# Attention scores of 128 queries computed as two halves of 64 queries by 192 keys

## The chip, the core and the metric

The kernel runs on one core of a Trainium2 chip. A core has a tensor engine (PE in the profile; its weight loads are listed apart as PEld), a vector engine (DVE), a scalar engine (ACT), GpSimd (POOL) and a sync engine (SP) that issues most transfers; 16 DMA engines move the data. The metric is device time in microseconds (us) of the one core, the median of several executions, and lower is better.

## The reference

One inference step of a small decoder: a pooling layer, then an attention layer, over a prompt of 1024 tokens and 8 single decode tokens, all in fp32 with a model width of 2048. The part that matters here is the attention of the prompt. There are 32 query heads of 64 dimensions over 4 key/value heads, and the window is 128: in blocks of 128 queries, each query sees keys of its own block up to itself and keys of the block before that are less than 128 back.

```python
def attn_core(q, k, v, q_pos, k_pos, sinks):
    s = jnp.einsum('...qkgd,...skd->...kgqs', q, k).astype(jnp.float32) * (HEAD_DIM ** -0.5)
    qp = q_pos[..., :, None]
    kp = k_pos[..., None, :]
    mask = (kp <= qp) & (qp - kp < WINDOW) & (kp >= 0)
    s = jnp.where(mask[..., None, None, :, :], s, NEG)
    sink = sinks.astype(jnp.float32).reshape(N_KV_HEADS, GROUP)[:, :, None, None]
    m = jnp.maximum(jnp.max(s, axis=-1, keepdims=True), sink)
    p = jnp.exp(s - m)
    p = p / (jnp.sum(p, axis=-1, keepdims=True) + jnp.exp(sink - m))
    return jnp.einsum('...kgqs,...skd->...qkgd', p.astype(v.dtype), v)
```

The keys of a block of 128 queries are 256: the 128 of the block before (slots 0 to 127) and its own 128 (slots 128 to 255). Query i of the block may use slot k of the block before only where k > i, and slot k of its own only where k <= i, so exactly 128 of the 256 scores of a query are used.

## The kernel before

The tokens are worked on in two chunks of 512 and 520 (512 prompt tokens and 8 decode tokens). The large projections are matrix products with fp32 operands split into a high and a low part, three products each (lines 654 to 656 of `seven`, a Strassen scheme with seven block products; lines 682 to 684 of `unit`, a plain scheme for two short stages). The phases run in the order of the table `PHASES`: "ai" (input projection of the pooling layer), "ao" (its output), "bi" (key/value, query and gate projections of the attention layer, with the attention itself between them), "bo" (its output), each for chunk 0 and chunk 1. The first half of "bi" for chunk 0 is a plain phase, the rest Strassen.

The order on PE, DVE and ACT is the order of the source: `in_order` chains each instruction of these three engines to the one before it. SP's and POOL's queues are left to the scheduler of the framework. What work of the attention goes where between the projections is written out with counters: `self.at(n, go)` runs `go` n steps of the projection later, `self.product(n, rank, go)` does the same for work on PE, at the end of a step. Each `end()` closes a step.

`attend` handles two heads (one tile of 128 channels, head j in partitions 64j to 64j+63) over the four blocks of a chunk. Its pieces: `score` (line 1755) multiplies queries by keys into the PSUM tile `S`, of 2 by 1024 floats per partition, head j in half j, block b in columns 256b to 256b+255. `select` (line 1772, ACT) copies slots 0 to 127 of each block out of `S`; `largest` (line 1776, DVE) copies the block's own slots over them where the mask `mki` says k <= i, so that 128 scores are left for each query, and takes the maximum; exponentials and division follow (lines 1789 to 1804); `turn` (line 1808, PE) transposes the result back into `S`; `keep` (lines 1817 and 1818) copies it out; `values` (line 1832, PE) multiplies by the values, for head j into partitions 64j to 64j+63, and `gate` (line 1841) multiplies with the gate. There are 16 calls of `attend` per chunk, 32 in all.

`S` is made once, when the "bi" stage of chunk 0 opens (`use_four(False)`); `kv_open` sets up the key and value tiles there. The first other writer of `S` is `v_done` (line 1681), which transposes values into half 0; decode scores use `S` too (line 1926).

The prediction also speaks of line 593 (an ACT operation on the Strassen accumulators that PE waits for), line 1620 (rotary embedding on DVE), lines 490 and 774 (DVE, low parts of weights and activations), line 1966 (values of the decode tokens).

Of the kernel before, what the change touches and what calls it, by code (L numbers as in the profile page):

```python
# [16 lines left out]
P = 128  # L17
# [164 lines left out]
class Kern:  # L182
# [1439 lines left out]
    def kv_open(self, c):  # L1622
        nc = self.nc
        T = CHUNKS[c][1]
        if c == 0:
            self.kv = [self.mem.full() for _ in range(4)]
            A, B, C, Dd = (s.a for s in self.kv)
            self.kT = [A[:, :640], B[:, :640]]
            self.vd = B[:, 640:896]
            self.V = [A[:, 640:896]] + [C[:, b * 256 : (b + 1) * 256] for b in range(4)]  # L1630
            self.Vd = [Dd[:, b * 256 : (b + 1) * 256] for b in range(4)]
            for k in self.kT:
                nc.gpsimd.memset(k[:, 0:P], 0.0)
            nc.gpsimd.memset(self.V[0], 0.0)
            self.rt = self.mem.full()
        else:

            def over():
                for k in self.kT:
                    nc.scalar.copy(k[:, 0:P], k[:, TP : TP + P])  # L1640
                nc.scalar.copy(self.V[0], self.V[NB])

            self.at(6, over)
        self.rtab = self.rt.v(2, TMAX)
        nc.sync.dma_start(self.rtab[:, :, :T], self.io[f"rt{c}"])
# [95 lines left out]
    def attend(self, c, t, at, s1, s2, late=False):  # L1741


        nc = self.nc
# [5 lines left out]
        def score():  # L1750
            s, q, lastq = self.qs.pop((c, t))
            for b in range(NB):
                for j in range(2):
                    r = slice(64 * j, 64 * j + 64)
                    nc.tensor.matmul(  # L1755
                        self.S[:, j, b * 256 : b * 256 + 256], q[r, b * P : (b + 1) * P],
                        self.kT[t // 8][r, b * P : b * P + 256], start=True, stop=True,
                    )
            if lastq:
                s.free()  # L1760

# [76 lines left out]
        def gate():  # L1838
# [13 lines left out]
            if j == 1 or t == 15 or self.sg.get((c, t + 1), (None,))[0] is not z:  # L1852
                z.free()

        self.product(at, 2, score)
        for n, go in enumerate((
            select, largest, lambda: expo(0), lambda: expo(1), total, lambda: norm(0), lambda: norm(1)
# [466 lines left out]
```

## Time and profile before

| | |
|---|---|
| median of 3 runs | 2366.13 us (2365.59 to 2367.04) |
| the profiled execution, its own time | 2367.1 us |
| its span, first to last instruction | 2365.3 us |
| mean granted TensorE clock | 0.997 |
| PE busy | 98% of the span |
| DVE busy | 81% |
| ACT busy | 58% |
| score products, line 1755 | 512 matmul records, 63.9 us busy |

Times in the profile are us from the start of the span unless marked ns. A matmul's record is longer than the time after which the next one can start, since matmuls are pipelined; the pace is therefore read from starts, not from durations. In a row of the timeline, "x16" says that 16 instructions of one line that follow each other are merged: the first number is the start of the first, the second the time to the end of the last. Shapes such as "64\*128 64x256" of a matmul mean: weights of 64 rows (partitions) and 128 columns, moving data of 64 partitions by 256 elements.

### The profile page before, as it was taken

The numbers are of one execution on the slowest core, as the hardware profiler recorded it, in microseconds if no ns is written. First come the engines' busy times: TensorE is split into PE (matmuls) and PEld (weight loads), VectorE is DVE, ScalarE is ACT, GpSimd is POOL, SyncE is SP. The second block draws the span as 40 slices with busy tenths as digits, with TensorE's granted clock in tenths as the row PEclk, the third lists the DMA queues.
The fourth block names the chain that finished last, engine by engine and source line by source line (L and its number), as shares of the span: only waits on it lengthen the run. The fifth ranks groups of instructions, "written<-read, shape, count | busy, mean of one in ns | idle before, by whom it ended". The sixth has DMA issues, their size and how long they took to land. (4 is left out here: it accounts for less than half of the span.)

```text
span 2365.3 us, 46576 instructions
## 1 busy us (share of the span) xinstructions
PE 2325.4 (98%) x18424; PEld 2218.8 (94%) x18424; DVE 1922.8 (81%) x2385; ACT 1364.2 (58%) x2502; POOL 201.8 (9%) x379
## 2 busy tenths in 40 slices
PE   8999999999999999999999999999999999999997
PEld 6899999999999999998778899999999999999997
DVE  8788988776878878868888897887777767888887
ACT  4454446544546547554554666675666678556656
POOL 0111110001000000000111111100000000000000
PEclk9999999999999999999999999999999999999999
DMA  8668789989879889989789776788776768699785
GB/s 292 214 243 303 269 289 340 338 286 321 294 279 363 320 279 326 336 313 330 280 317 332 258 239 216 242 290 269 240 256 220 225 191 296 229 350 362 272 303 194
DMA packets 252060, 669.19 MB, mean 283 GB/s; under 512 B 25760, under 2 KB 106560, under 8 KB 251840
## 3 DMA queue, kind: packets, MB, share of 16 engines
q1 hardware_dynamic: 206368, 501.14, 63.0%
q0 software_dynamic: 45472, 165.07, 18.0%
q8 instruction: 144, 2.36, 0.4%
q14 instruction: 76, 0.62, 0.1%
HBM read 471.01 MB, written 185.59 MB: 278 GB/s over the span
## 5 line engine op out<-in xcount | busy, mean ns | idle before, releaser
L654 PE MATMUL pD<-m,m 128*128 128x260 f32 (+1 forms) x4752 | 1346.1, 283 | 7.9 <-ACT pD L593 5.7
L656 PE MATMUL pD<-m,m 128*128 128x260 f32 (+1 forms) x4752 | 1340.2, 282 | 6.9 <-DVE m L490 6.8
L655 PE MATMUL pD<-m,m 128*128 128x260 f32 (+1 forms) x4752 | 1339.5, 282 | 0.9 <-DVE m L774 0.9
L654 PEld LDWEIGHTS pD<-m,m 128*128 128x128 f32 x4752 | 895.1, 188 | 18.6 <-issue 8.0
L656 PEld LDWEIGHTS pD<-m,m 128*128 128x128 f32 x4752 | 895.7, 188 | 9.2 <-DVE m L490 9.2
L655 PEld LDWEIGHTS pD<-m,m 128*128 128x128 f32 x4752 | 895.5, 188 | 1.6 <-DVE m L774 1.1
L490 DVE TENSOR_TENSOR m<-m,m 128x1024 fp32r<-128x1024 f32 x674 | 814.4, 1220 | 87.2 <-ACT m L475 55.1
L475 ACT CAST m<-m 128x1024 fp32r<-128x1024 f32 x674 | 703.6, 1048 | 266.2 <-DVE m L333 66.6
L682 PE MATMUL pD<-m,m 128*128 128x512 f32 x448 | 179.9, 402 | 8.1 <-ACT m L765 8.1
L683 PE MATMUL pD<-m,m 128*128 128x512 f32 x448 | 177.5, 396 | 0.5 <-DVE m L774 0.5
L684 PE MATMUL pD<-m,m 128*128 128x512 f32 x448 | 177.5, 396 | 0.0
L774 DVE TENSOR_TENSOR m<-m,m 128x1024 fp32r<-128x1024 f32 (+1 forms) x120 | 147.2, 1228 | 7.4 <-ACT m L765 6.0
L765 ACT CAST m<-m 128x1024 fp32r<-128x1024 f32 (+1 forms) x120 | 125.8, 1053 | 15.0 <-PE pD L683 5.2
L615 DVE TENSOR_TENSOR m<-pD,m 128x260 f32<-128x260 f32 (+1 forms) x86 | 36.6, 425 | 107.5 <-ACT pD L614 100.0
L627 ACT COPY m<-pD 128x260 f32<-128x260 f32 (+1 forms) x83 | 31.0, 374 | 153.4 <-PE pD L656 153.4
L682 PEld LDWEIGHTS pD<-m,m 128*128 128x128 f32 x448 | 84.8, 189 | 30.0 <-ACT m L765 8.1
L333 DVE TENSOR_TENSOR m<-m,m 128x1024 f32<-128x1024 f32 x88 | 107.6, 1222 | 5.8 <-DMA m<-in_wia 4.3
L683 PEld LDWEIGHTS pD<-m,m 128*128 128x128 f32 x448 | 84.9, 190 | 19.9 <-DVE m L774 1.0
L684 PEld LDWEIGHTS pD<-m,m 128*128 128x128 f32 x448 | 84.8, 189 | 19.9
L1791 ACT ACTIVATE m<-m,sm 128x128 f32<-128x128 f32 x256 | 99.2, 390 | 0.0
L1084 PE MATMUL pD<-m,m 128*128 128x260 f32 (+1 forms) x528 | 91.5, 323 | 0.0
L1084 PEld LDWEIGHTS pD<-m,m 128*128 128x128 f32 x528 | 79.5, 188 | 8.2
(244 smaller groups left out, 2151.4 us busy)
## 6 DMA issues: line engine op xcount, KB each, us to landing
m<-in_wia SPq DMA_DIRECT2D x124, 512.0 KB
m<-in_wib SPq DMA_DIRECT2D x120, 512.0 KB
swia<-m POOLq DMA_DIRECT2D x64, 512.0 KB, 4.8
m<-swia SPq DMA_DIRECT2D x64, 512.0 KB
m<-swoa SPq DMA_DIRECT2D x64, 512.0 KB
swib<-m POOLq DMA_DIRECT2D x64, 512.0 KB, 5.2
m<-swib SPq DMA_DIRECT2D x64, 512.0 KB
m<-swob SPq DMA_DIRECT2D x56, 512.0 KB
```

Of the source, the lines that this page charges most:

```text
L333: self.nc.vector.tensor_add(s[out].a[:, :1024], s[x].a[:, :1024], s[y].a[:, :1024])
L475: self.nc.scalar.copy(hi.r[:, :1024], self.stream[self.cast].src().a[:, :1024])
L490: self.nc.vector.tensor_sub(lo.r[:, :1024], s.src().a[:, :1024], hi.a[:, :1024])
L654: nc.tensor.matmul(ps[:, :TH], wh[:, s], h, start=new and k == 0, stop=False, skip_group_check=on)
L655: nc.tensor.matmul(ps[:, :TH], wh[:, s], l, start=False, stop=False, skip_group_check=on)
L656: nc.tensor.matmul(ps[:, :TH], wl[:, s], h, start=False, stop=k == 7, skip_group_check=on)
L682: nc.tensor.matmul(ps[:], wh[:, s], h, start=par == 0 and k == 0, stop=False)
L683: nc.tensor.matmul(ps[:], wh[:, s], l, start=False, stop=False)
L684: nc.tensor.matmul(ps[:], wl[:, s], h, start=False, stop=par == 1 and k == 7)
L765: self.nc.scalar.copy(h.r[:, :n], s.a[:, :n])
L774: self.nc.vector.tensor_sub(l.r[:, :n], s.a[:, :n], h.a[:, :n])
L1084: nc.tensor.matmul(ps[:, : cs.stop - cs.start], ws[:, s], d[:, cs], start=f0 and k == 0, stop=l0 and k == 3,)
```

## The change

Each product of 128 queries by 256 keys is replaced by two: queries 0 to 63 by slots 0 to 191, and queries 64 to 127 by slots 64 to 255. Head j lies in partitions 64j to 64j+63 of the operands, half a of the queries in partitions 64a to 64a+63 of the result, so the four combinations of j and a use four different quarters (64 rows by 64 columns) of the PE array. For each block there are four such products where there were two. The scores left out are those of queries 0 to 63 with slots 192 to 255 and of queries 64 to 127 with slots 0 to 63. None of them is used by the mask; the places in `S` keep what was there. `select` still copies slots 0 to 127 of all queries, and `largest` overwrites the old content in slots 0 to 63 of the upper queries. So that nothing unset is read, half 1 of `S` is set to zero once by DVE, 4 steps after the stage opens.

```diff
@@ kv_open, chunk 0 @@
             for k in self.kT:
                 nc.gpsimd.memset(k[:, 0:P], 0.0)
+            self.at(4, lambda: nc.vector.memset(self.S[:, 1, :], 0.0))
             nc.gpsimd.memset(self.V[0], 0.0)
@@ attend, score @@
             for b in range(NB):
                 for j in range(2):
                     r = slice(64 * j, 64 * j + 64)
-                    nc.tensor.matmul(
-                        self.S[:, j, b * 256 : b * 256 + 256], q[r, b * P : (b + 1) * P],
-                        self.kT[t // 8][r, b * P : b * P + 256], start=True, stop=True,
-                    )
+                    for a in range(2):
+                        h, k = 64 * a, b * P + 64 * a
+                        nc.tensor.matmul(
+                            self.S[h : h + 64, j, b * 256 + h : b * 256 + h + 192], q[r, k : k + 64],
+                            self.kT[t // 8][r, k : k + 192], start=True, stop=True,
+                        )
```

## The prediction

> **What bounds the kernel now.** I read the head of the page first, then the busy time of the engines over the attention stage, cut in three, and what PE waited for there.
>
> ```profile
> PE 2325.4 (98%) x18424; PEld 2218.8 (94%) x18424; DVE 1922.8 (81%) x2385; ACT 1364.2 (58%) x2502; POOL 201.8 (9%) x379
> ```
>
> ```profile
> core 0: us, PE busy (x) PEld busy (x) DVE busy (x) ACT busy (x) POOL busy (x), PEclk, DMA share, GB/s
> 1150.00:1345.00 195.00, 193.51 (x1059) 155.61 (x1058) 169.06 (x237) 110.75 (x261) 33.95 (x66) 1.00 0.85 305
> 1345.00:1610.00 265.00, 260.77 (x2335) 251.96 (x2335) 230.38 (x275) 181.97 (x413) 28.24 (x56) 1.00 0.74 251
> 1610.00:2060.00 450.00, 447.08 (x4035) 432.68 (x4034) 330.50 (x428) 303.13 (x704) 24.41 (x39) 1.00 0.72 236
> ```
>
> ```profile
> PE pD L654 <- ACT pD L593: 3.6, 4, 1.2
> PE pS L1755 <- DVE m L1727: 1.5, 1, 1.5
> PE pD L656 <- DVE m L490: 0.9, 2, 0.5
> ```
>
> PE is the bound. Over these 910 us it is idle for 1.49 + 4.23 + 2.92 = 8.6 us; DVE, the next, is busy 87%, 87% and 73% of the three windows, no transfer is among PE's longer waits, and the clock is granted in full. So PE time saved on the scores is device time, except where PE soon waits for another engine anyway. Such places lie in the second window.
>
> **What a burst of scores costs now.** The first rows below give all records of line 1755; the others are rows of the PE timeline: two bursts with what follows them, and, from narrow windows, starts inside the first burst of all.
>
> ```profile
> L1755 PEld LDWEIGHTS pS<-m,m x512: 182/187/187, 1159.1 to 2009.9; 64*128 64x128 f32 x171
> L1755 PE MATMUL pS<-m,m x512: 376/376/481, 1159.1 to 2010.1; 64*128 64x256 f32 x171
> ```
>
> ```profile
> 1159.40 0.59 PE L1755 MATMUL pS<-m,m 64*128 64x256 f32 x3
> 1159.62 0.59 PE L1755 MATMUL pS<-m,m 64*128 64x256 f32 x3
> ...
> 1160.48 0.59 PE L1755 MATMUL pS<-m,m 64*128 64x256 f32 x3
> ...
> 1675.61 1.97 PE L1832 MATMUL pO<-m,m 128*64 128x128 f32 x32
> 1677.50 2.00 PE L1755 MATMUL pS<-m,m 64*128 64x256 f32 x16
> 1679.43 0.39 PE L654 MATMUL pD<-m,m 128*128 128x260 f32 x1
> ```
>
> 512 records over 32 calls are 16 per burst, where the code issues 8 products: an fp32 product is two passes. A burst holds PE from 1677.50 to 1679.43, 1.93 us. A record takes 376 ns; 16 in a row would be 6.0 us. Starts inside the burst come 0.22 us apart (1159.40, 1159.62), five steps taking 1.08 us (1159.40 to 1160.48), so a step is 0.216 us. Eight steps are 1.73 us: two records go in each step, one per head, on the upper and the lower half of the array's rows, and 1.93 - 1.73 = 0.20 us are filling and draining. The value products of line 1832 halve the array the other way (weights of 128 rows by 64 columns): 32 records of 128 moving columns in 1.89 us (1675.61 to 1677.50). In 16 steps of two that is at most 1.89 / 16 = 0.118 us a step, or 0.108 if a step costs half of 0.216 for half the columns; one by one they would need at least 32 times that, some 3.5 us. So two halves of rows do run together, and so do two halves of columns.
>
> **The change, part by part.**
>
> *The scores.* Per burst, 8 products of 256 columns become 16 of 192, that is 32 records. A step of 192 columns is 0.216 x 192 / 256 = 0.162 us. The trace has no array in four quarters, so I bound it.
> - Four together: 32 / 4 = 8 steps, 8 x 0.162 + 0.20 = 1.50 us, 0.43 less than now. If filling shrinks too (line 1832 leaves 1.89 - 16 x 0.108 = 0.16 us), 0.47 less.
> - Two together: 16 steps, 2.59 + 0.20 = 2.79 us, 0.86 more than now.
>
> I take four, 0.43 us, since both directions of the cut are each shown. The Trainium skill (TensorEngine Tiling (Array Packing), Tiling Modes) lists 64x64 as four tiles that work independently; by it the sum would be the same, and no run here has shown it yet.
>
> *Weights and issue.* Weight loads double to 32 per burst, with half the columns. The products of the decode values show the price of so many:
>
> ```profile
> 1839.10 1.01 PEld L1966 LDWEIGHTS pO<-m,m 128*64 128x64 f32 x32
> ...
> 1839.10 1.10 PE L1966 MATMUL pO<-m,m 128*64 128x8 f32 x32
> 1840.13 0.39 PE L654 MATMUL pD<-m,m 128*128 128x260 f32 x1
> ```
>
> 32 loads of 64 columns and 32 matmuls take 1.03 us (1839.10 to 1840.13) when there are only 8 columns to stream. That is under 1.50, so neither loading nor issue sets the pace even if the loads pass one after the other. Cost: nothing, covered by the streaming.
>
> *How much arrives.* 32 bursts, but not all on the path. The chain of waits through one of the Strassen steps of chunk 0, with the burst that lies beside it:
>
> ```profile
> 1427.34 0.13 PE pD L655
> 1427.71 0.98 issue
> 1428.69 2.36 DVE m L1620 x2
> ...
> 1442.07 1.27 DVE m L1776
> 1443.36 1.23 DVE sm L1780
> ...
> 1445.22 1.54 ACT m L1791 x8
> 1446.76 0.28 ACT pD L593
> 1447.08 0.39 PE pD L654
> ```
>
> ```profile
> 1432.36 2.00 PE L1755 MATMUL pS<-m,m 64*128 64x256 f32 x16
> 1434.29 0.38 PE L654 MATMUL pD<-m,m 128*128 128x256 f32 x1
> ```
>
> From 1427.7 to 1447.1 the path is on DVE and ACT, and PE stalls at its end for line 593 (up to 1.2 us). The burst at 1432.36 is inside, so its saving only lengthens that stall. The waits of PE in the window from 1345 to 1610 us alone say how often:
>
> ```profile
> PE pD L654 <- ACT pD L593: 2.8, 3, 1.2
> PE pD L655 <- DVE m L774: 0.9, 1, 0.9
> ```
>
> The same holds at the two other waits for line 593, and at the one for line 774, the end of a DVE stretch that lies behind a burst too. I count 4 bursts as lost, 4 x 0.43 = 1.7 us. The other 28 count: 28 x 0.43 = 12.0 us. What is late next is then ACT's line 593 and DVE, in chunk 0 alone.
>
> *The zeroing.* One DVE operation on 128x1024 of PSUM, which stands just before a product of line 280 (1093.34, two of them). DVE rows on the score tile, and DVE's next idle times:
>
> ```profile
> L1818 DVE TENSOR_TENSOR m<-pS,cst x32: 1219/1225/1226, 1201.5 to 2045.2; 128x1024 f32<-128x1024 f32 x32
> ...
> L1932 DVE COPY m<-pS x4: 216/218/225, 1793.8 to 2035.5; 128x64 f32<-128x64 f32 x4
> ```
>
> ```profile
> 1107.79 1.23 DVE L490 TENSOR_TENSOR m<-m,m 128x1024 fp32r<-128x1024 f32 x1 [1.39 <-ACT m L475]
> ...
> 1112.77 1.23 DVE L1620 TENSOR_TENSOR m<-m,m 128x1024 f32<-128x1024 f32 x1 [2.49 <-DMA m<-m]
> ```
>
> Between 0.22 and 1.23 us; by size it is nearest line 1818. Behind it on DVE stand weight and layer-norm pieces, for which PE could wait; the 1.39 + 2.49 us idle up to 1112.8 absorb it, so nothing, or 1.2 us once if a piece before 1107 is urgent.
>
> *Queues.* PE, ACT and POOL keep their order but for the changed products, and DVE only gains the zeroing. On SP five transfers (weight loads, rotary swaps and loads for sums) change places with near neighbours. Weight loads are not waited for in this stage: nothing, within some tenths either way.
>
> *After the attention.*
>
> ```profile
> 2060.00:2200.00 140.00, 135.28 (x1130) 134.04 (x1130) 123.68 (x140) 82.26 (x111) 9.58 (x18) 1.00 0.99 354
> ```
>
> In the output projection the 16 DMA engines are full and PE is idle 4.7 us. Those loads are issued as PE frees tiles, so the stage should start 12 us earlier and last as long; at worst some 2 us more of waiting comes back.
>
> **The sum.** The profiled execution took 2367.1 us (span 2365.3), 1.0 us above the median of 2366.13. From it 2367.1 - 12.0 = 2355.1; against the median 2354.1 us, 0.51% less. Bounds while four run together: 32 x 0.47 = 15.0 us if every burst counts and filling shrinks, and 12.0 - 1.2 - 2 = 8.8 us with zeroing and later waits against it, so 2351 to 2357.5.
>
> **The rivals.**
>
> *Two quarters at a time (slower).* One mechanism at line 1755: if PE can't look far enough ahead in its queue to fill four quarters, or only two of them stream at once, a burst is 2.79 us. 0.86 us on 28 bursts is 24 us, and the other 4 bursts fall beside stalls of about 1 us: 2366.1 + 24 = 2390 us. It decides as soon as a burst needs more than 1.93 us, which is 1.73 / 0.162 = 10.7 steps instead of 8. For it: the first pass of the fourth quarter stands behind six passes of the others, further than now. Against it: each two-way cut shows no such limit.
>
> *Strict order (slower).* The two passes of a product use the same quarter; if the second held back all behind it, only neighbours would overlap: 32 records in 17 steps, 17 x 0.162 + 0.20 = 2.95 us, 1.02 us more on 28 bursts, 2395 us. Against it: with this rule a burst now would take 9 steps, 1.94 us and filling, and the last start would come at least 8 x 0.216 = 1.73 us after the first; it comes 2.00 - 0.376 = 1.62 us after. This is the rule of the Trainium skill (TensorE: Matmul & The Clock Gate, Part 3, The mechanism: matmuls start and end in program order, "strict FIFO, no reordering"). On the rows just named the trace disagrees.
>
> *Nothing comes of it.* If a step stays 0.216 us, because four streams or four loads get in each other's way, 8 steps are 1.73 us again and the time is 2366. Against it: the 1.03 us burst above. A gain eaten by DVE (87% busy) would end in the same place; for that the 8.6 us of PE idling would have to more than double.
>
> **How the numbers follow.** A change under 0.2% (4.7 us) can't be told from none. Four together: 0.78, of which 0.74 between 2351 and 2357.5 and 0.04 with more eaten, up to 2361. Nothing comes of it: 0.08. Two at a time 0.11 and strict order 0.03, slower by 24 to 29 us. The predicted time is the first case's, 2354.1; the range has to reach over the case of no change to hold 8 in 10, so 2350.5 to 2368, while the likeliest case's own range is 2351 to 2357.5. Faster 0.78, same 0.08, slower 0.14.
>
> **What would show it.** In the profile after: 32 records of 64x192 per burst, about 0.16 us between starts of four; from the first of a burst to the next projection product 1.50 us; PE's waits for line 593 about 0.4 us longer each; no PE wait near 1095 to 1115 us that wasn't there. The prediction is wrong if a burst takes over 1.9 us, or if bursts shrink and PE's idle time in the three windows grows by more than some 3 us.

## The result

The changed kernel takes 2355.8 us (median of 5 runs, 2353.8 to 2357.1) where the kernel before takes 2366.13: 10.3 us less, a ratio of 0.9955 with a 95% interval of 0.9941 to 0.9970. The forecast was 2354.1, with 2351 to 2357.5 for its likeliest case. The profiled execution has a span of 2355.0 us and took 2356.8, 1.0 us above its median, as the profiled execution before is above its own.

The burst of scores, first in the rows of line 1758 (the score line of the changed kernel), then in the PE timeline; the last row is from a narrow window 0.16 to 0.18 us into the burst:

```profile
L1758 PEld LDWEIGHTS pS<-m,m x1024: 129/133/133, 1158.7 to 1999.1; 64*64 64x64 f32 x171
L1758 PE MATMUL pS<-m,m x1024: 322/323/374, 1158.7 to 1999.3; 64*64 64x192 f32 x171
```

```profile
1673.09 1.53 PE L1758 MATMUL pS<-m,m 64*64 64x192 f32 x32
1674.55 0.39 PE L654 MATMUL pD<-m,m 128*128 128x260 f32 x1
...
1673.09 0.39 PE L1758 MATMUL pS<-m,m 64*64 64x192 f32 x4
```

32 records in 1.46 us (1673.09 to 1674.55), where 16 took 1.93. The last starts 1.53 - 0.323 = 1.21 us after the first; 32 records one by one would need 10.3 us. The first four records last 0.373 us each and the last of them ends 0.39 us after the first began, so they start within 0.02 us of each other. Four quarters of the array stream together, and 0.47 us is saved per burst, 32 x 0.47 = 15.0 us in all. So 4.7 us of the saving didn't arrive. Busy time by window, and what PE waited for in the attention stage:

```profile
core 0: us, PE busy (x) PEld busy (x) DVE busy (x) ACT busy (x) POOL busy (x), PEclk, DMA share, GB/s
1150.00:1345.00 195.00, 193.33 (x1208) 156.12 (x1210) 171.54 (x240) 113.63 (x267) 33.95 (x66) 1.00 0.87 311
1345.00:1610.00 265.00, 258.60 (x2476) 250.93 (x2469) 230.36 (x276) 180.96 (x410) 28.96 (x57) 0.99 0.74 250
1610.00:2060.00 450.00, 446.85 (x4350) 434.34 (x4349) 338.88 (x435) 304.72 (x707) 24.76 (x40) 1.00 0.75 243
```

```profile
PE pD L654 <- ACT pD L593: 5.0, 4, 1.7
PE pS L1758 <- DVE m L1728: 1.7, 2, 1.5
PE pD L655 <- DVE m L774: 1.1, 1, 1.1
```

PE's idle time grew mostly in the second window, from 4.2 to 6.4 us (in the others by 0.2 us each), and the wait for line 593 over the whole stage from 3.6 to 5.0. Where the saving stays away is seen best in the starts of the bursts. The first, eighth, ninth, sixteenth and last in the kernel before:

```profile
1159.11 2.00 PE L1755 MATMUL pS<-m,m 64*128 64x256 f32 x16 [1.49 <-DVE m L1727]
1347.75 2.00 PE L1755 MATMUL pS<-m,m 64*128 64x256 f32 x16
1384.99 2.00 PE L1755 MATMUL pS<-m,m 64*128 64x256 f32 x16
1560.48 2.00 PE L1755 MATMUL pS<-m,m 64*128 64x256 f32 x16
2008.50 2.00 PE L1755 MATMUL pS<-m,m 64*128 64x256 f32 x16
```

and in the changed kernel (bursts 1 to 16 belong to chunk 0, 17 to 32 to chunk 1):

```profile
1158.73 1.53 PE L1758 MATMUL pS<-m,m 64*64 64x192 f32 x32 [1.49 <-DVE m L1728]
1344.41 1.53 PE L1758 MATMUL pS<-m,m 64*64 64x192 f32 x32
1383.64 1.53 PE L1758 MATMUL pS<-m,m 64*64 64x192 f32 x32
1557.45 1.53 PE L1758 MATMUL pS<-m,m 64*64 64x192 f32 x32
1998.06 1.53 PE L1758 MATMUL pS<-m,m 64*64 64x192 f32 x32
```

| from start of burst | bursts between | saving due | lead gained | lost |
|---|---|---|---|---|
| 1 to 8 | 7 | 3.3 | 0.38 to 3.34: 3.0 | 0.3 |
| 8 to 9 | 1 | 0.5 | 3.34 to 1.35: -2.0 | 2.5 |
| 9 to 16 | 7 | 3.3 | 1.35 to 3.03: 1.7 | 1.6 |
| 16 to 32 | 16 | 7.5 | 3.03 to 10.44: 7.4 | 0.1 |
| 32 to the end of the span | 1 | 0.5 | 10.44 to 10.3: -0.1 | 0.6 |

All numbers of the table are us, from one execution of each kernel; the lead is how much earlier a burst starts than in the kernel before. In chunk 1 everything arrives, in chunk 0 less than half. Between 1350 and 1380 us even an older lead is given back. The PE timeline of the changed kernel there, and the windows of just that stretch (the second lies in the output projection):

```profile
1357.95 0.38 PE L654 MATMUL pD<-m,m 128*128 128x256 f32 x1 [0.49 <-ACT pD L614]
1359.41 0.53 PE L655 MATMUL pD<-m,m 128*128 128x256 f32 x1 [1.07 <-DVE m L774]
1359.74 0.42 PE L656 MATMUL pD<-m,m 128*128 128x256 f32 x1
1359.96 0.41 PE L654 MATMUL pD<-m,m 128*128 128x256 f32 x1
...
1363.06 0.28 PE L654 MATMUL pD<-m,m 128*128 128x256 f32 x1
1363.18 0.28 PE L655 MATMUL pD<-m,m 128*128 128x256 f32 x1
```

```profile
1359.50:1362.90 3.40, 3.40 (x16) 3.40 (x17) 3.40 (x4) 1.35 (x8) 0.00 (x0) 0.50 0.51 208
2137.80:2141.10 3.30, 3.26 (x15) 3.26 (x16) 2.65 (x4) 1.04 (x1) 0.00 (x0) 0.50 1.05 400
```

The kernel before ran 29 matmuls at full clock in the stretch that answers to the first of these:

```profile
1362.30:1365.70 3.40, 3.40 (x29) 3.40 (x30) 3.40 (x4) 1.42 (x8) 0.00 (x0) 1.00 0.92 265
```

What DVE had gained by then is read where it last waited, through a copy on ACT, for a product of PE, between bursts 6 and 7 (line 1818, 1821 in the changed kernel). First that operation and PE's restart behind line 774 before, then the operation after:

```profile
1310.97 1.22 DVE L1818 TENSOR_TENSOR m<-pS,cst 128x1024 f32<-128x1024 f32 x1 [4.05 <-ACT m L1817]
1362.28 0.39 PE L655 MATMUL pD<-m,m 128*128 128x256 f32 x1 [0.89 <-DVE m L774]
...
1308.11 1.23 DVE L1821 TENSOR_TENSOR m<-pS,cst 128x1024 f32<-128x1024 f32 x1 [4.05 <-ACT m L1820]
```

DVE is 2.86 us ahead there, and PE restarts behind line 774 with a lead of 1362.28 - 1359.41 = 2.87 us: what bursts 7 and 8 saved is gone. So two things are lost between bursts 8 and 9: the lead above DVE's own, 3.34 + 0.47 - 2.87 = 0.9 us, and then about 1.5 us in which the granted clock is 0.50 and matmuls start 0.22 us apart instead of 0.12. The half clock costs 13 of 29 matmuls, 13 x 0.12 = 1.5 us.

### The profile page after: what moved, and what is told of

Same layout as the page of the kernel before. It is cut to its first block, busy times and chain, and to the rows that moved or that the text cites. A ratio compares the mean times of both kernels' runs of the same rounds, so it can differ in the third digit from the quotient of the medians.

```text
span 2355.0 us, 47605 instructions
## 1 busy us (share of the span) xinstructions
PE 2313.7 (98%) x18936; PEld 2211.4 (94%) x18936; DVE 1924.1 (82%) x2386; ACT 1364.5 (58%) x2502; POOL 202.2 (9%) x379
```

## The experiments

My theory: four quarters go together at the pace of the streamed columns; what is lost is lost in chunk 0, where PE waits for stretches of DVE and of ACT behind DVE, and to the clock after such a wait. Rivals: the zeroing costs time; the gain isn't from the columns left out; the loss is spread over all bursts or lies after the attention.

**The zeroing left out.**

```diff
-            self.at(4, lambda: nc.vector.memset(self.S[:, 1, :], 0.0))
...
+                    if c == 0 and t == 0:
+                        nc.tensor.matmul(
+                            self.S[:, j, b * 256 : b * 256 + 256], q[r, b * P : (b + 1) * P],
+                            self.kT[t // 8][r, b * P : b * P + 256], start=True, stop=True,
+                        )
+                        continue
                     for a in range(2):
```

> The changed kernel without the zeroing of half 1 of the score tile; instead the first of the 32 score bursts is the old one (8 products of 128 by 256), which writes the whole tile. If the zeroing costs nothing, as the DVE rows after it say (0.91 us at 1094, made up by 1107), the time stays within 1 us of the changed kernel (2355.8), 0.5 us of it for the one old burst. If the zeroing is what took part of the gain, the time falls by 1 us or more.

2354.72 us (2354.1 to 2358.0), ratio 0.9954 with an interval of 0.9939 to 0.9969, the changed kernel's within noise. The median is 1.1 us lower, just what the expectation would have put down to the zeroing, but it lies far inside the interval: no cost of the zeroing can be told from none, and the DVE rows shown further down say that there is none. In this execution PE waited for lines 614 and 774 just as long near 1359 us, but the clock stayed at 1.00:

```profile
PE pD L655 <- DVE m L774: 1.1, 1, 1.1
PE pD L654 <- ACT pD L614: 0.5, 1, 0.5
```

```profile
1358.00:1363.00 5.00, 4.59 (x39) 4.59 (x40) 4.97 (x6) 1.86 (x9) 0.66 (x2) 1.00 0.55 206
```

Bursts 8 and 9 start at 1343.40 and 1381.11 us here, so the lead falls from 4.35 to 3.88 us: 0.9 us is lost, where the changed kernel with its stretch of half clock lost 2.5.

**All 256 keys on the quarters.**

```diff
-                            self.S[h : h + 64, j, b * 256 + h : b * 256 + h + 192], q[r, k : k + 64],
-                            self.kT[t // 8][r, k : k + 192], start=True, stop=True,
+                            self.S[h : h + 64, j, b * 256 : b * 256 + 256], q[r, k : k + 64],
+                            self.kT[t // 8][r, b * P : b * P + 256], start=True, stop=True,
```

> Queries still in two halves on four quarters, but each half against all 256 keys. Four quarters going together: a step is 0.216 us again, 8 steps and less filling, a burst of about 1.89 us instead of 1.93 before and 1.46 in the changed kernel; the time is 2364 to 2366. If the gain came from the quarters themselves (cheaper loads, shorter start and end) and not from the 64 columns left out, a burst would stay near 1.5 us and the time near 2356. Only two quarters at a time: 16 steps, 3.6 us a burst, over 2400.

2365.91 us, ratio 1.0000 (0.9991 to 1.0009). A burst of this kernel in the PE timeline:

```profile
1676.55 1.96 PE L1758 MATMUL pS<-m,m 64*64 64x256 f32 x32
1678.43 0.39 PE L654 MATMUL pD<-m,m 128*128 128x260 f32 x1
```

1.88 us, as eight steps of 0.216 and 0.16 make 1.89. The cut into quarters by itself is worth 0.05 us a burst, and nothing that the medians can tell; it pays because it allows a quarter of the columns to be left out.

**One chunk alone.** In the score loop, for chunk 1 alone (for chunk 0 alone the condition is `c == 1`):

```diff
+                    if c == 0:
+                        nc.tensor.matmul(
+                            self.S[:, j, b * 256 : b * 256 + 256], q[r, b * P : (b + 1) * P],
+                            self.kT[t // 8][r, b * P : b * P + 256], start=True, stop=True,
+                        )
+                        continue
                     for a in range(2):
```

> Quarters in the 16 bursts of chunk 1 only, the old products in chunk 0. If all of the saving arrives in chunk 1, 16 x 0.467 = 7.5 us less than before, 2358.7. If the loss is spread evenly over all bursts, 5.2 us less, 2361.

> Quarters in the 16 bursts of chunk 0 only, the old products in chunk 1. If DVE and ACT stretches in chunk 0 eat the saving, 16 x 0.467 = 7.5 us shrinks to 3 to 5 us, 2361 to 2363, 1.5 us of it hanging on whether the granted clock drops after the stall near 1360 us. If the loss is spread evenly, 5.2 us less, 2361; if it lies after the attention, 7 us less, 2359.

Chunk 1 alone: 2358.86 us, ratio 0.9973 (0.9960 to 0.9985), 7.2 us less than the kernel before beside it (2366.06), of 7.5 possible. Chunk 0 alone: 2363.22, 0.9986 (0.9976 to 0.9995), 2.8 us less, a little less gain than I expected. By the intervals alone (3.5 to 9.5 us and 1.2 to 5.7 us less) 5.2 us in each would still be possible; the starts of the bursts rule it out. With chunk 1 alone, burst 17 starts at 1629.44 us (1630.13 before) and burst 32 at 2000.76 (2008.50 before): the lead grows by 7.05 us over 15 bursts, all that is due. With chunk 0 alone, burst 1 starts at 1156.86 and burst 16 at 1556.47: it grows by 1.8 of 7.0 us. The loss is in chunk 0; an even spread and a loss after the attention are out.

The clock isn't needed for such a loss: in the execution with chunk 0 alone it is 1.00 throughout the attention. A wait stands at the sixth burst instead that the changed kernel's execution doesn't have, for DVE's rotary embedding:

```profile
1290.13 1.53 PE L1764 MATMUL pS<-m,m 64*64 64x192 f32 x32 [1.52 <-DVE m L1728]
```

So where in chunk 0 the saving is lost differs between executions.

**Another order of the quarters.**

```diff
-            for b in range(NB):
-                for j in range(2):
-                    r = slice(64 * j, 64 * j + 64)
-                    for a in range(2):
+            for a in range(2):
+                for j in range(2):
+                    r = slice(64 * j, 64 * j + 64)
+                    for b in range(NB):
```

> The changed products in another order: all four blocks of one quarter of the array first, then the next quarter. If PE can look past the 16 instructions of a quarter for work of the others, a burst stays near 1.46 us. If it sees only a few instructions ahead, the quarters go one after the other: 32 steps of 0.162 us, 5.3 us a burst, 32 x 3.8 = 122 us more, 2478. In strict order the same.

2414.78 us in one run, 49 us slower than the kernel before, between the two expectations. A burst of it, after a product of the plain stage; the last row is from a narrow window, with what had started in the first 0.71 us:

```profile
1213.44 3.63 PE L1758 MATMUL pS<-m,m 64*64 64x192 f32 x32
1217.00 0.51 PE L682 MATMUL pD<-m,m 128*128 128x512 f32 x1
...
1213.44 1.08 PE L1758 MATMUL pS<-m,m 64*64 64x192 f32 x6
```

3.56 us. One quarter after the other would be 32 x 0.162 + 0.16 = 5.3 us, all together 1.46. The 2.1 us between 3.56 and 1.46, over three changes of quarter, are 0.70 us each, 4.3 steps. The starts in the trace say the same: the first five records start 0, 0.21, 0.38, 0.54 and 0.70 us into the burst, and the sixth at 0.71, too soon for a step of 0.162 us on the same quarter, so it is the next quarter's first; the other two quarters follow at 1.41 and 2.12 us. A quarter starts while three of the eight records of the quarter before it are still to start. So PE does pass work that waits for its own quarter, but here it passed only about three matmuls; what sets that limit these runs don't show. The order in the change, where a quarter never has more than two records in a row, needs no more.

**DVE made lighter in chunk 0**, before and after. The maximum is taken over 16 of the 128 scores of a query there, so part of the maximum is left out.

```diff
-            nc.vector.tensor_reduce(mx[:], s3, axis=AX.X, op=ALU.max)
+            nc.vector.tensor_reduce(mx[:], s3 if c else s3[:, :, :16], axis=AX.X, op=ALU.max)
```

> The kernel before, with the maximum of chunk 0 taken over 16 of the 128 scores of a query only: part of the computation is left out, about 1.0 us of DVE work in each of 16 calls. PE's waits on ACT's line 593 and on line 774 (3.7 us) go away or shrink: 2362 to 2365.

> The changed kernel with the same 16-score maximum in chunk 0, so the same part left out. If the DVE stretches of chunk 0 (and the clock drop that follows a stall there) are what ate 4.6 us of the 14.9, this kernel is 13 to 15 us below the kernel before with the short maximum, near 2349 to 2351. If the loss lies elsewhere, the difference stays near 10.3 us.

Without the change 2363.96 us (0.9989, 0.9979 to 0.9998), with it 2351.17 (0.9934, 0.9920 to 0.9948): 12.8 us apart, where it was 10.3. That lies just below my 13 to 15. PE's waits in the window from 1345 to 1610 us, all of them, in the changed kernel with the short maximum:

```profile
PE pD L654 <- ACT pD L593: 1.4, 2, 0.7
PE pD L642 <- ACT m L627: 0.5, 1, 0.5
```

The wait for line 774 is gone, and PE waits 1.4 us for line 593 instead of 4.2; without the change it waits 0.5 us for it there, instead of 2.8. By the medians about half of the loss comes back with 0.93 us less of DVE work in 16 places, but their intervals are 4.5 and 6.6 us wide, so these 2.5 us aren't clear of noise. The traces bear it out in part. From burst 1 to 16 the lead over the kernel before with the same maximum grows by 4.9 of 7.0 us (these two start at 1158.05 and 1555.91 us there, at 1157.36 and 1550.31 here), where it had grown by 2.65; of these 2.3 us more, 1.5 are the stretch of half clock, which this execution doesn't have; that leaves some 0.8 us for the lighter DVE.

**Line 593 ahead of the exponentials.** In the Strassen steps of chunk 0's attention stage, its ACT operation, which follows the first of the seven block products, is issued at the end of that product, before the other work of the step, instead of at the start of the next step.

```diff
             if idx in after:
                 self.posts.append(after[idx])
+            if idx == 0 and self.ph == "bi0":
+                self.flush()
             self.end()
```

> The kernel before, with one order on ACT changed in the Strassen steps of chunk 0's attention stage: the operation of line 593 stands ahead of the exponentials (which wait for DVE's maximum) instead of behind them. PE waits for it 2.8 us in all there; if the exponentials in front of it are the cause, these waits go and the time falls by up to 2.8 us, 2363 to 2364. If line 593 isn't held by them, no change.

> The changed kernel with the same change of order. PE's waits for line 593 in the second window are 4.2 us; without them the savings of the three bursts beside them arrive too (1.4 us) and the old 2.8 us as well, unless DVE itself is next: 2351 to 2353. The wait for line 774 at about 1359 us stays, and with it the chance of a clock drop there.

The kernel before gains: 2364.18 us, 0.9989 (0.9981 to 0.9998), 2.3 us. The changed one is at 2354.05, 0.9948 (0.9934 to 0.9961), one to three microseconds short of what I expected, and its interval overlaps that of the changed kernel alone. In both, PE's wait for line 593 is gone; the two longest that are left in the second window, in the changed kernel:

```profile
PE pD L655 <- DVE m L776: 1.1, 1, 1.1
PE pD L656 <- DVE m L490: 1.0, 2, 0.5
```

(line 776 is line 774 shifted by the edit). The exponentials in front of line 593 were the cause of that wait. But the change gains no more by its going: with line 593 early it is worth 2364.18 - 2354.05 = 10.1 us, as it was 10.3 with the old order. The order helps both kernels about alike; the wait for line 774 stays, and one for line 490 comes in.

**Eighths.** Groups of 32 queries by 160 keys, on eight parts of 64 rows by 32 columns, with the order on ACT as it was, and then with line 593 early.

```diff
-                    for a in range(2):
-                        h, k = 64 * a, b * P + 64 * a
+                    for a in range(4):
+                        h, k = 32 * a, b * P + 32 * a
                         nc.tensor.matmul(
-                            self.S[h : h + 64, j, b * 256 + h : b * 256 + h + 192], q[r, k : k + 64],
-                            self.kT[t // 8][r, k : k + 192], start=True, stop=True,
+                            self.S[h : h + 32, j, b * 256 + h : b * 256 + h + 160], q[r, k : k + 32],
+                            self.kT[t // 8][r, k : k + 160], start=True, stop=True,
```

> The cut taken further: four groups of 32 queries by 160 keys each, on eight parts of 64 rows by 32 columns. Eight together: 8 steps of 160 x 0.844 = 0.135 us, 1.08 us and about 0.15, a burst of 1.2 to 1.25 us, 0.2 to 0.25 less than the quarters; with the share that arrived there (0.69) 4.5 to 5.5 us less than the changed kernel, 2350 to 2351.5. If 64 loads and 64 matmuls are too many to issue in 1.2 us (the only row has 32 and 32 in 1.03 us, which would make 2.06), a burst is over 2 us and the time over 2366.

> Eighths (32 queries by 160 keys) with the same change of order. Bursts of 1.25 us; all 16 savings in chunk 1 (16 x 0.68 = 10.9 us) and, if the waits for line 593 were the eater in chunk 0, most of 10.9 there too, less some 2 to 4 us for the stretch up to line 774: 2347 to 2350, the fastest. If DVE is the bound of chunk 0's stage whatever the order on ACT, it stays near 2352 to 2354.

A burst of the eighths:

```profile
1673.74 1.32 PE L1758 MATMUL pS<-m,m 64*32 64x160 f32 x64
1674.99 0.39 PE L654 MATMUL pD<-m,m 128*128 128x260 f32 x1
```

1.25 us, as expected, 0.21 less than the quarters. Alone it gives 2354.03 us, 0.9948 (0.9935 to 0.9960), of the changed kernel's 0.9955 hardly apart, against 2350 to 2351.5 expected. In its profile PE waits 4.8 us for line 593 and 1.6 us for line 1728 in the second window, and the clock is at half twice in chunk 0, again just behind waits of PE:

```profile
1357.30:1360.60 3.30, 3.08 (x14) 3.08 (x15) 3.30 (x5) 1.67 (x9) 0.00 (x0) 0.50 0.49 199
1497.20:1500.40 3.20, 3.20 (x17) 3.20 (x17) 2.83 (x5) 2.44 (x9) 0.53 (x1) 0.50 0.78 314
```

With line 593 early it is 2347.75 us (2346.9 to 2349.2), 0.9923 (0.9910 to 0.9935): 18.7 us less than the kernel before beside it (2366.49), the fastest of all, and within what was expected of it; 2.3 us of that is what the order gives the kernel before. The other 16.4 us are what eighths gain beside the kernel before with the same order, of 32 x 0.68 = 21.8 due, so chunk 0 still eats a part. Line 593 is no longer among PE's waits. The order is worth 2.3 us before the change, about 1.7 with quarters and about 6 with eighths (from the ratios), and of the 6 some 1.5 may be the clock, since the eighths' profile has one stretch of half clock more in chunk 0 without it than with it.

## Why the prediction was right, point by point

- *Four together.* Right. Eight steps per burst, 1.46 us where 1.50 was taken and 1.46 the better end; filling did shrink to 0.16 us. The term was 0.43 us and measured 0.47.
- *Weights and issue.* Right: 32 and even 64 loads and matmuls per burst are covered.
- *How much arrives.* The mechanism was right and its size off. I let 4 bursts be eaten, 1.7 us. In the profile 4.1 us are lost from burst 8 to burst 16: three waits for line 593 (1.6 us, where the step said 3 x 0.43; in their window they went from 2.8 to 4.2 us, 0.47 each), but at the stretch before line 774 not one burst but 2.5 us. That stretch, which DVE has to finish first, took back all the lead that PE had gained since DVE's last wait for a product of PE, and that was two bursts, 0.9 us; the prediction counted the bursts inside the chain's rows only. The rest of the 2.5 us is the clock, which the prediction hadn't at all.
- *The zeroing.* Right; it took 0.91 us between the two bounds, and DVE made it up. No PE wait came in near 1095 to 1115 us:

```profile
1094.39 0.91 DVE L1634 MEMSET pS<- 128x1024 f32 x1 [0.21 <-issue]
...
1107.41 1.23 DVE L490 TENSOR_TENSOR m<-m,m 128x1024 fp32r<-128x1024 f32 x1 [0.42 <-ACT m L475]
```

DVE's wait there shrank from 1.39 to 0.42 us.
- *After the attention.* About right: 0.6 us came back, less than the 2 us allowed, with one half-clock stretch among it (2137.8 us).
- *The rivals.* Two at a time and strict order are out by the 1.46 us burst. Strict order is also out by the other order of the quarters: 3.56 us where it makes 5.3, with the next quarter's first product started before the last three records of the quarter ahead of it. The Trainium skill's rule (TensorE: Matmul & The Clock Gate, Part 3, The mechanism) doesn't hold between quarters here. A weaker form of it is real, the three or so matmuls that PE passed.

The sum was 1.7 us too optimistic: the bursts save 32 x 0.04 = 1.3 us more, but 5.1 us are lost by the table instead of 1.7, and 0.4 us were ahead before the first burst: 12.0 + 1.3 - 3.4 + 0.4 = 10.3 us. That it came so close is in part luck: the loss was 3.4 us larger than forecast, and half of that was made up by shorter bursts and by a head start that no step had forecast. PE's idle time in the three windows is 1.7 + 6.4 + 3.2 = 11.2 us, 2.6 more than before, just under the 3 at which the prediction called itself wrong; the stretch of half clock isn't in it, since PE is busy there.

## What to carry to other kernels

Cutting a small matmul into quarters of the array was worth next to nothing by itself; it pays when the cut lets streamed columns be left out, as the corners of a band mask do, and when consecutive products alternate between the parts. On a PE that is busy 98% the saving is worked out per stage: it arrives in full where PE never waits, and a stretch in which another engine must finish first takes back all that was gained since that engine last waited for a product of PE, as at line 774 here. Look for such stretches, and at the order on the other engine, before counting on the next cut: one operation moved on ACT gave about 6 us with the eighths, though with quarters no more than without.

## What the runs showed that was not expected

PE's granted clock halved for 3.4 us behind short waits, at an estimated 1.5 us each (the 13 matmuls above): in the changed kernel at 1359.5 us, behind waits of 0.49 and 1.07 us, in the eighths at 1357.2 and 1497.1 us, and in the eighths with line 593 early at 1357.9 us. In the kernel without the zeroing the same two waits left the clock at 1.00. The traces show where these two executions differ. Within a trace the stretches of half clock start whole multiples of 3.413 us apart: in the changed kernel at 362.81, 1359.50 and 2137.74 us, which is 292 and then 228 times 3.413. On this grid both waits of the changed kernel (the first two rows) fall into one window, and the half clock is the next; without the zeroing (the last two) a border at 1357.38 us parts them:

```profile
1356.09:1359.50 3.41, 1.85 (x14) 1.45 (x12) 3.41 (x4) 3.06 (x12) 0.53 (x1) 1.00 0.29 100
1359.50:1362.91 3.41, 3.41 (x16) 3.41 (x17) 3.41 (x4) 1.35 (x8) 0.00 (x0) 0.50 0.51 208
...
1353.97:1357.38 3.41, 2.87 (x23) 2.47 (x21) 3.33 (x6) 2.14 (x11) 0.00 (x0) 1.00 0.06 7
1357.38:1360.79 3.41, 2.38 (x20) 2.38 (x21) 3.41 (x4) 2.48 (x9) 0.53 (x1) 1.00 0.82 297
```

PE idles 1.56 us in the one window, 0.54 and 1.03 us in the two. In the 13 traces of this document, without the first 15 and the last 20 us of each, PE idled 1.8 us or more in 14 windows of this grid at full clock, and the clock halved behind every one; between 1.55 and 1.76 us it did so behind 2 of 13, below that never. So it seems to be the idle time summed up in one window that counts, and not the longest single wait; no run was made to test it, and near 1.6 us it stays open which way it goes. The Trainium skill (TensorE: Matmul & The Clock Gate, Part 1) describes a window of about 3.4 us that runs freely, and the grid in the traces agrees. Nor had I expected that the order of the same products could more than double a burst.
